# A pad of 128 bytes behind the constants of a two-layer SSD and attention trunk

## The chip, the core and the metric

The kernel runs on one core of one Trainium2 chip. The core has a matrix engine (TensorE, PE in the profile; its weight loads are shown apart as PEld), a vector engine (VectorE, DVE), a scalar engine (ScalarE, ACT), GpSimd (POOL), and a queue processor (SyncE, SP) that here issues nearly all transfers. The transfers are carried by 16 DMA engines from device memory to the on-chip memory of 128 partitions. The metric is the time of one execution on the device in microseconds (us).

## The reference

The model takes `x` (256 tokens by 2048) and a vector `c`, and runs two layers in float32, with one shared key and value projection between them. Cut to what matters:

```python
for layer in range(2):
    shift, scale, gate = split(silu(c) @ ada_w[layer] + ada_b[layer], 3)    # adaLN
    h = x * (1 + scale) + shift
    if layer == 0:   # SSD mixer: 64 heads of 64, 8 groups, state 128
        z, xBC, dt = split(h @ a_in_w)                    # 2048 x 10304
        xs, B, C = split(silu(causal_conv4(xBC)))
        y = ssd_scan(xs * softplus(dt), softplus(dt) * -exp(A_log), B, C) + D * xs
        y = group_rmsnorm(y * silu(z)) * norm_g @ a_out_w  # 4096 x 2048
    else:            # dilated window attention: 3 groups of 8 heads of 128
        q, z = split(h @ b_in_w)                          # 2048 x 4096
        o = merge_by_lse(attention(q_g, k_g, v_g, window_g, dilation_g) for g in 3 groups)
        y = (o * silu(z)) @ b_out_w                       # 1024 x 2048
    x = layer_norm(alpha * x + (1 + gate) * y)
    if layer == 0:
        k, v = split(x @ kv_w)                            # 2048 x 6144, once
```

## The kernel before

Nearly all of the time goes into products of the 256 tokens with float32 weights. Each weight matrix lies in device memory in pieces of 128 partitions by 1024 numbers (4 KB to a partition). A piece is loaded into a tile `raw` (line 89, six buffers), then split into two parts in the matmul format float32r: ACT writes the high part `whi` (line 99) and DVE writes `wlo` = raw - whi (line 101). The activations are split in the same way, and a product is the sum of three matmuls: high by high, high by low, low by high. There are two ways to run it:

- Token-major (`tm_mults`, lines 212 to 214): the activations are the stationary operand and the weights the moving one, 512 columns at a time. The z products of layer 0, `wout`, the v products and `wbout` run so.
- Channel-major: the weights are stationary, and the activations move. In `cm_piece` (lines 150 to 152) 256 columns move in each of the three matmuls. In `cm_wide` (lines 181 and 184) high and low activations lie side by side, so that 512 columns move past the high weights, and then 256 past the low ones. `wxs`, k, q and the gate of layer 1 run so.

The tiles `whi` and `wlo` are 1088 numbers long, and a piece begins at one of two places in them: at number 0 (`LONG`) where it will be the moving operand, or at number 16, 64 bytes further on (`SHORT`), where it will be stationary.

```python
    SHORT, LONG = (16, 16), (0, 0)
    ...
        return [wp.tile([P, 1088], F32R, name=n, bufs=4)[:, o:o + 1024] for n, o in zip(("whi", "wlo"), off)]
    ...
        copied.append(S.activation(hi, raw, AF.Copy))
        ...
            latest.append(V.tensor_tensor(lo, raw, hi.bitcast(F32), op=ALU.subtract))
```

AdaLN is not a matmul. Its weights (96 rows of 1 MB, 8 KB to a partition, tile `araw`, issued at line 287) are multiplied by silu(c), which stands in the constant tile `cb_` on every partition, and summed by one DVE instruction a row (line 294). Layer 0's shift and scale must be known before `h`, so 32 of these rows come first, and the opening of the kernel (to about 160 us) weaves them with the first weight pieces by a list written out by hand. Later rows are worked off in the background between pieces. The order of every engine is the order in which the program issues the work; some instructions are pinned behind others by `tc.issue_after`. All weight and adaLN transfers go through SP's queue, and each waits for its buffer to come free.

The tiles come from pools that lie behind each other in the on-chip memory, each tile at a multiple of 32 bytes. First come the constants (pool `cons`): `cb_` (8192 bytes to a partition), `adab` (384), `prm` (1732), `cc` (1536; identity, triangle, ones), and further on in the code `magic` and the two `mod` tiles of the adaLN results. Behind them lie the weights (`wp`), the activations (`act`), small tiles (`sm`), the slots, and the pools that come and go with the stages. Only the residual `u` (pool `pu`) is laid out from the other end.

```python
    cb_ = cons.tile([P, D], F32, name="cb_")
    ...
    adab_ = cons.tile([P, NB], F32, name="adab")
    prm = cons.tile([P, NPAR - NB], F32, name="prm")
    ...
    cc = cons.tile([P, NCONST], F32, name="cc")
    ...
    ident = cc[:, CI:CI + 128]
    tri = cc[:, CT:CT + 128]
    ones = cc[:, CM:CM + 128]
```

Of the kernel before, what the change touches and what calls it, by code (L numbers as in the profile page):

```python
# [9 lines left out]
F32 = mybir.dt.float32  # L10
# [8 lines left out]
P = 128  # L19
# [30 lines left out]
def trunk(ctx, tc, xT, x, c, par, cst, bias, lnrow, ada, wdt, win, wxs, wout, wk, wv, wbin, wbout, out):  # L50
# [3 lines left out]
    cons = ctx.enter_context(tc.tile_pool(name="cons", bufs=1))  # L54
# [23 lines left out]
    ident = cc[:, CI:CI + 128]  # L78
    tri = cc[:, CT:CT + 128]
    ones = cc[:, CM:CM + 128]  # L80
    SHORT, LONG = (16, 16), (0, 0)

    def rows(t, b):
# [1293 lines left out]
```

## Time and profile before

| | |
|---|---|
| median of 3 runs | 1236.28 us (1235.71 to 1237.11) |
| profiled execution | 1236.29 us, span 1234.5 us |
| granted TensorE clock, mean | 0.999 |
| moved by DMA | 335.92 MB, mean 272 GB/s |
| DMA busy share, main queue | 75.0% of 16 engines |

The span is the time from the first to the last instruction of the profiled execution; 1.8 us of its time lie around it. Busy time of an engine is the time in which at least one of its instructions ran. A row of a group of instructions gives its line, engine, operation, output and inputs, shapes and count, then the busy time and the mean duration of one, then the idle time of the engine just before them. Consecutive matmuls overlap, so the mean duration of one is longer than the distance between two starts. Line numbers are those of the kernel before.

### The profile page before, as it was taken

What the parts mean: (1) busy time and instruction counts of PE and PEld (TensorE: products, weight loads), DVE (VectorE), ACT (ScalarE), POOL (GpSimd) and SP (SyncE); (2) the same over time, 40 slices, a digit from 0 to 9 for tenths busy, and PEclk for the clock granted to TensorE, in tenths of its full rate; (3) what the DMA queues carried; (4) which work ended last, traced back from release to release, by engine and by line L of the source; (5) the groups of instructions that cost most, each with busy time, mean ns of one, the idle gap of its engine ahead of it and who ended that gap; (6) DMA issues with size and microseconds to landing.
All of it is one profiled execution on the core that took longest, in us unless ns stands there. A gap on an engine that the chain in (4) does not pass through costs nothing.

```text
span 1234.5 us, 18854 instructions
## 1 busy us (share of the span) xinstructions
PE 1220.3 (99%) x7132; PEld 1049.4 (85%) x7132; DVE 1028.0 (83%) x1464; ACT 701.6 (57%) x1048; POOL 3.9 (0%) x8
## 2 busy tenths in 40 slices
PE   8999999999999999999999999999999999999998
PEld 7889988898888888888888788888888888888886
DVE  6899996999988989899778678888978876758776
ACT  3554577878597789754335545344445644445551
POOL 0000000000000000000000000000000000000001
PEclk9999999999999999999999999999999999999999
DMA  9999986687666456599998569989998774464673
GB/s 373 414 414 415 413 283 244 216 305 247 222 204 205 171 172 205 203 337 353 365 316 294 195 204 362 356 341 371 378 382 313 224 261 147 122 201 124 207 256 69
DMA packets 81372, 335.92 MB, mean 272 GB/s; under 512 B 9201, under 2 KB 9985, under 8 KB 68481
## 3 DMA queue, kind: packets, MB, share of 16 engines
q1 hardware_dynamic: 80352, 333.33, 75.0%
q0 software_dynamic: 576, 1.05, 0.6%
q8 instruction: 56, 0.92, 0.3%
q10 hardware_dynamic: 352, 0.34, 0.1%
q14 instruction: 36, 0.29, 0.1%
HBM read 331.45 MB, written 3.23 MB: 271 GB/s over the span
## 4 chain that ended last, share of the span: by engine, by line
PE 84%; DMA 6%; DVE 6%; ACT 2%; issue 1%; ACTq 0%; DVEq 0%
PE acc L181 24%; PE acc L184 12%; PE acc L213 12%; PE acc L214 12%; PE acc L212 12%; DMA raw<-in_win 5%; DVE araw L294 3%; DVE wlo L101 2%; PE py L775 1%; PE acc L150 1%; PE acc L152 1%; PE acc L151 1%; DMA araw<-in_ada 1%; ACT whi L99 1%; PE acc L985 1%
## 5 line engine op out<-in xcount | busy, mean ns | idle before, releaser
L99 ACT ACTIVATE whi<-raw 128x1024 fp32r<-128x1024 f32 x389 | 408.9, 1058 | 362.5 <-PE acc L214 130.7
L101 DVE TENSOR_TENSOR wlo<-raw,whi 128x1024 fp32r<-128x1024 f32 x389 | 469.2, 1221 | 146.8 <-ACT whi L99 139.9
L181 PE MATMUL acc<-actT,whi 128*128 128x512 f32 x1280 | 402.8, 394 | 0.0
L184 PEld LDWEIGHTS acc<-actT,wlo 128*128 128x128 f32 x1280 | 239.5, 188 | 53.5 <-DVE wlo L101 0.5
L213 PE MATMUL acc<-wlo,actT 128*128 128x512 f32 x656 | 257.3, 392 | 1.9 <-DVE wlo L101 1.9
L212 PE MATMUL acc<-whi,actT 128*128 128x512 f32 x656 | 254.0, 394 | 0.0
L184 PE MATMUL acc<-actT,wlo 128*128 128x256 f32 x1280 | 253.8, 280 | 0.0
L294 DVE SCALAR_TENSOR_TENSOR araw<-araw,cb__72 128x2048 f32<-128x2048 f32 x95 | 217.0, 2284 | 5.2 <-DMA araw<-in_ada 4.7
L181 PEld LDWEIGHTS acc<-actT,whi 128*128 128x128 f32 x1280 | 193.9, 188 | 0.4
L214 PE MATMUL acc<-whi,actT 128*128 128x512 f32 x432 | 168.8, 391 | 0.0
L213 PEld LDWEIGHTS acc<-wlo,actT 128*128 128x128 f32 x656 | 123.2, 188 | 28.7 <-DVE wlo L101 3.6
L212 PEld LDWEIGHTS acc<-whi,actT 128*128 128x128 f32 x656 | 122.6, 188 | 25.1 <-ACT s L634 0.8
L150 PE MATMUL acc<-actT,whi 128*128 128x256 f32 x372 | 103.7, 283 | 2.9 <-ACT s L634 2.0
L152 PE MATMUL acc<-actT,wlo 128*128 128x256 f32 x372 | 102.4, 283 | 1.7 <-DVE wlo L101 1.6
L151 PE MATMUL acc<-actT,whi 128*128 128x256 f32 x372 | 103.6, 281 | 0.0
L214 PEld LDWEIGHTS acc<-whi,actT 128*128 128x128 f32 x432 | 81.1, 188 | 16.6
L214 PE MATMUL acc<-whi,ylo 128*128 128x512 f32 x224 | 87.6, 391 | 0.0
L150 PEld LDWEIGHTS acc<-actT,whi 128*128 128x128 f32 x372 | 70.3, 190 | 4.2 <-ACT s L634 2.4
L152 PEld LDWEIGHTS acc<-actT,wlo 128*128 128x128 f32 x372 | 69.5, 190 | 2.7 <-DVE wlo L101 2.7
L151 PEld LDWEIGHTS acc<-actT,whi 128*128 128x128 f32 x372 | 71.3, 192 | 0.2
L214 PEld LDWEIGHTS acc<-whi,ylo 128*128 128x128 f32 x224 | 42.1, 188 | 8.7
L733 ACT ACTIVATE seg<-cbc,cumT 128x128 f32<-128x128 f32 x128 | 41.1, 390 | 2.6 <-PE py L775 2.1
(311 smaller groups left out, 1151.1 us busy)
## 6 DMA issues: line engine op xcount, KB each, us to landing
araw<-in_ada SPq DMA_DIRECT2D x96, 1024.0 KB, 7.4
raw<-in_win SPq DMA_DIRECT2D x109, 512.0 KB, 5.7
raw<-in_wout SPq DMA_DIRECT2D x64, 512.0 KB, 5.8
raw<-in_wbin SPq DMA_DIRECT2D x64, 512.0 KB, 4.0
raw<-in_wxs SPq DMA_DIRECT2D x48, 512.0 KB, 4.4
raw<-in_wv SPq DMA_DIRECT2D x48, 512.0 KB, 6.8
raw<-in_wk SPq DMA_DIRECT2D x48, 512.0 KB, 7.2
cbc<-cumd SPq DMA_DIRECT2D x16, 512.0 KB, 4.9
```

What stands on the lines that cost most here:

```text
L99: copied.append(S.activation(hi, raw, AF.Copy))
L101: latest.append(V.tensor_tensor(lo, raw, hi.bitcast(F32), op=ALU.subtract))
L150: T.matmul(o, hi[:, k, c_], ahi[:, kt, :], start=first, stop=False, skip_group_check=True)
L151: T.matmul(o, hi[:, k, c_], alo[:, kt, :], start=False, stop=False, skip_group_check=True)
L152: T.matmul(o, lo[:, k, c_], ahi[:, kt, :], start=False, stop=kt == k1 - 1, skip_group_check=True)
L181: T.matmul(ps[n], hi[:, k, n * P:n * P + P], both(kt), start=kt == 0, stop=False, skip_group_check=True)
L184: T.matmul(ps[n][:, 0, :], lo[:, k, n * P:n * P + P], high(kt), start=False, stop=kt == KT - 1, skip_group_check=True)
L212: T.matmul(o, h_, hi[:, k, :], start=kt == k0, stop=False, skip_group_check=part)
L213: T.matmul(o, h_, lo[:, k, :], start=False, stop=False, skip_group_check=part)
L214: end = T.matmul(o, l_, hi[:, k, :], start=False, stop=kt == k1 - 1, skip_group_check=part)
L294: return V.scalar_tensor_tensor(raw, raw, 1.0, cb_, op0=ALU.mult, op1=ALU.mult, accum_out=mod[layer][:, ct, j:j + 1])
L733: S.activation(seg[:, hh, b, :], cbc[:, hh, b, :], AF.Relu, bias=cumT[:, b, h0 + hh:h0 + hh + 1], scale=-1.0)
```

## The change

One tile of 32 float32 numbers, 128 bytes on each partition, is added to the pool of constants behind `cc`. No instruction writes it or reads it.

```diff
     ident = cc[:, CI:CI + 128]
     tri = cc[:, CT:CT + 128]
     ones = cc[:, CM:CM + 128]
+    cons.tile([P, 32], F32, name="pad")
     SHORT, LONG = (16, 16), (0, 0)
```

Everything that is laid out behind it lies 128 bytes further on. The table gives where tiles begin, as the remainder by 256 bytes:

| tiles | before | after |
|---|---|---|
| `cb_`, `adab`; `prm`; `cc` | 128; 0; 224 | 128; 0; 224 |
| `raw`, `whi` and `wlo` (as tiles), activations `actT`, slots `s0` to `s7` | 128 | 0 |
| stationary weights, at `SHORT` in `whi` and `wlo` | 192 | 64 |
| moving weights, at `LONG` | 128 | 0 |
| `araw`, opening: pool `wp1`; pool `pe` | 128; 192 | 0; 64 |
| `araw`, later | 128 | 0 |
| `xt` and `htmp` of the opening | 192 | 64 |
| `xs`, `cbc`, `seg`, `sz`, `ylo`, `q`, `bs`, `pT`, `sc` | 128 | 0 |
| `u0`, `u1` | 224 | 224 |

The instructions, their order on each engine and queue, their waits and their shapes are the same in both programs; only addresses differ, and each line number behind the pad is larger by one.

## The prediction

> **What bounds the kernel now.** I read the page's first part and the chain first: they say whose time the span is.
>
> ```profile
> span 1234.5 us, 18854 instructions
> PE 1220.3 (99%) x7132; PEld 1049.4 (85%) x7132; DVE 1028.0 (83%) x1464; ACT 701.6 (57%) x1048; POOL 3.9 (0%) x8
> PE 84%; DMA 6%; DVE 6%; ACT 2%; issue 1%; ACTq 0%; DVEq 0%
> ```
>
> TensorE (PE) is busy for 1220.3 of 1234.5 us and makes 84% of the chain; the DMA's 6% and VectorE's (DVE) 6% can only lie where PE is not full. So next come busy times by stretch: the opening in pieces of 20 us, then a stretch of one v product and the wide k products.
>
> ```profile
> 20.00:40.00 20.00, 17.58 (x113) 16.28 (x114) 16.46 (x17) 12.02 (x18) 0.00 (x0) 0.91 1.02 414
> 40.00:60.00 20.00, 19.09 (x135) 17.02 (x135) 18.25 (x21) 9.90 (x14) 0.00 (x0) 1.00 1.02 414
> 60.00:80.00 20.00, 19.21 (x107) 16.36 (x107) 18.88 (x21) 11.65 (x15) 0.00 (x0) 1.00 1.02 413
> 80.00:100.00 20.00, 20.00 (x116) 17.58 (x115) 18.85 (x23) 10.75 (x14) 0.00 (x0) 1.00 1.02 413
> 100.00:120.00 20.00, 20.00 (x127) 18.11 (x126) 18.74 (x20) 10.64 (x15) 0.00 (x0) 1.00 1.02 415
> 120.00:140.00 20.00, 20.00 (x171) 19.85 (x170) 18.72 (x22) 8.49 (x11) 0.00 (x0) 1.00 1.02 414
> 140.00:160.00 20.00, 19.34 (x152) 18.45 (x152) 18.78 (x19) 10.51 (x13) 0.00 (x0) 1.00 1.01 402
> ...
> 740.00:900.00 160.00, 160.00 (x887) 139.03 (x886) 139.14 (x142) 70.70 (x88) 0.00 (x0) 1.00 0.94 361
> ```
>
> The columns are the stretch and its length, then the busy time of PE, weight loads (PEld), DVE, ACT and POOL, the granted clock, the DMA share and GB/s. From 20 to 140 us all sixteen DMA engines are full (share 1.02, 413 to 415 GB/s), yet PE itself is full from 80 to 140. From 740 to 900 PE has no gap at all. So there are two levers only: the pace of a matmul, nearly everywhere, and the transfers, in the opening, by as much as PE lacks there.
>
> A busy PE need not run at one pace, so the third look is at starts in the timeline. The first rows are the wout product (stationary activations, weights as the 512 moving columns), the next the wide k and v product (stationary weights), the last two the first product early and at 59 us.
>
> ```profile
> 600.17 0.39 PE L213 MATMUL acc<-wlo,actT 128*128 128x512 f32 x1
> ...
> 601.08 0.39 PE L214 MATMUL acc<-whi,ylo 128*128 128x512 f32 x1
> ```
>
> ```profile
> 771.37 0.40 PE L184 MATMUL acc<-actT,wlo 128*128 128x256 f32 x2
> ...
> 772.75 0.39 PE L184 MATMUL acc<-actT,wlo 128*128 128x256 f32 x2
> ```
>
> ```profile
> 22.18 0.28 PE L151 MATMUL acc<-actT,whi 128*128 128x256 f32 x1
> ...
> 22.52 0.28 PE L151 MATMUL acc<-actT,whi 128*128 128x256 f32 x1
> ```
>
> ```profile
> 59.34 0.28 PE L150 MATMUL acc<-actT,whi 128*128 128x256 f32 x1
> ...
> 59.81 0.28 PE L151 MATMUL acc<-actT,whi 128*128 128x256 f32 x1
> ```
>
> In wout four matmuls of 512 columns lie between the rows: 0.91 / 4 = 227.5 ns each. At 22 us three of 256 columns take 0.34 us, 113.3 ns each; at 59 us four take 0.47 us, 117.5 ns each. The wide product needs 1.38 / 2 = 690 ns for its set of four (two of 512, two of 256), where the paces above would give 2 x 227.5 + 2 x 113.3 = 681.7. So the same form runs at two paces some 4% apart, without any wait. What chooses between them no row says. That is the unknown of this case.
>
> **The change part by part.** *The pad itself.* Its tile is never written or read: on every engine and queue the same instructions stand in the same order with the same waits. Nothing is added or removed: 0 us, and no cover to lose.
>
> *Addresses of what PE reads.* Weights, activations and the slots move together by 128 bytes. The moving operand starts at 128 over a multiple of 256 now, and at 0 after; stationary weights with the SHORT offset of 64 bytes go from 192 to 64. The distance between the two operands of a matmul stays. The trace has one pair of neighbours: weight loads from 192 (L181, SHORT) and from 128 (L213, stationary activations).
>
> ```profile
> L181 PE MATMUL acc<-actT,whi 128*128 128x512 f32 x1280 | 402.8, 394 | 0.0
> L213 PE MATMUL acc<-wlo,actT 128*128 128x512 f32 x656 | 257.3, 392 | 1.9 <-DVE wlo L101 1.9
> L181 PEld LDWEIGHTS acc<-actT,whi 128*128 128x128 f32 x1280 | 193.9, 188 | 0.4
> L213 PEld LDWEIGHTS acc<-wlo,actT 128*128 128x128 f32 x656 | 123.2, 188 | 28.7 <-DVE wlo L101 3.6
> L151 PE MATMUL acc<-actT,whi 128*128 128x256 f32 x372 | 103.6, 281 | 0.0
> ```
>
> Both loads take 188 ns, and the matmuls around them 394 and 392. No moving operand of these lines starts anywhere but at 128, so the trace can't price the move to 0. The ends are the two paces: every matmul of the slower sort quickened, or every one of the quicker sort slowed. They are worked out as rivals below, about -10.0 and +8.9 us. I take 0, since a shift that both operands share leaves their distance alone and the nearest pair of addresses, 64 bytes apart, shows nothing.
>
> *Addresses of what ACT and DVE read and write.* The split of a weight piece writes wlo at 128 in wout's stretch (LONG) and at 192 in the wide one (SHORT).
>
> ```profile
> L101 DVE TENSOR_TENSOR wlo<-raw,whi x45: 1206/1225/1227, 570.6 to 687.6; 128x1024 fp32r<-128x1024 f32 x45
> ```
>
> ```profile
> L101 DVE TENSOR_TENSOR wlo<-raw,whi x47: 1217/1221/1226, 769.2 to 898.5; 128x1024 fp32r<-128x1024 f32 x47
> ```
>
> ```profile
> L101 DVE TENSOR_TENSOR wlo<-raw,whi 128x1024 fp32r<-128x1024 f32 x389 | 469.2, 1221 | 146.8 <-ACT whi L99 139.9
> ```
>
> The columns of the first two rows are minimum, median and maximum in ns. Medians of 1225 and 1221 ns mean that DVE hardly sees such offsets. If it did, by those 4 ns, 389 splits (the page's row) would be 1.6 us, either way. DVE is busy 83% of the span, so that lies beside matmuls; in the opening, where DVE has less room (16.5 to 18.9 of 20 us), a part of it could show. ACT, busy 57%, has more room than DVE for its half of the split. I put 0 for both.
>
> *Addresses that the transfers write.* Weight pieces (4 KB to a partition) and adaLN rows (8 KB) land at 128, the adaLN rows in the second pool of the opening at 192; after, at 0 and 64. Two short stretches hold almost nothing on the main queue but 8 KB rows, first into the pool at 128, then into that at 192.
>
> ```profile
> DMA packets 196, 0.83 MB, mean 415 GB/s; under 512 B 99, under 2 KB 99, under 8 KB 99
> q1 hardware_dynamic: 106, 0.79, 93.9%
> ```
>
> ```profile
> DMA packets 86, 0.64 MB, mean 426 GB/s; under 512 B 8, under 2 KB 8, under 8 KB 8
> q1 hardware_dynamic: 86, 0.64, 101.3%
> ```
>
> The first is 5.2 to 7.2 us: 196 - 99 = 97 rows of 8 KB in 0.939 x 16 x 2.0 = 30.0 us of engine time, 310 ns each. The second is 12.8 to 14.3 us: 86 - 8 = 78 rows in 1.013 x 16 x 1.5 = 24.3 us, 312 ns each. Moving the landing place by 64 bytes changes 0.6% at most. A landing at 0 is in neither. The ends: no gain, or all that PE lacks from 20 to 160 us, 140 - 135.22 (the sum of the seven rows) = 4.8 us and 9% of the clock for 20 us, 1.8 us, together -6.6 us. I take 0, by the pair of rows, which is nearest. Behind 160 us PE lacks little or other engines make the gap, and a quicker transfer is hidden by PE.
>
> The Trainium skill speaks for a gain here, in "DMA: Bandwidth & Descriptors", section "How a descriptor splits into AXI transactions": a descriptor that does not begin at a multiple of 256 bytes has its first transaction begin at the boundary below, and bytes that are fetched unused still cost beats. By its count a 4 KB row at 128 takes 132 beats where an aligned one takes 128, 3.0%, and an 8 KB row 260 for 256, 1.5%; at the opening's mixture some 2% of 140 us, an estimate of 3 us. By the rows the sum has 0 there. By the same count the row at 192 would be 0.8% dearer than that at 128, and 312 against 310 ns neither shows nor excludes that.
>
> The sum is 0. The profiled execution took 1236.29 us, its span 1234.5 and 1.8 around it; the median of the runs is 1236.28. I predict 1236.3 us.
>
> **The rivals.** *Quicker transfers (faster).* If landing at 0 makes rows 2% quicker, between the 0.6% of the pair and the 4.7% (6.6 of 140 us) behind which nothing is left to win, the full queue from 20 to 160 us delivers the last piece 2.8 us sooner, and PE's gaps can take it in: 1233.5 us. Over 0.2% it is worth from 1.8% on. Against it: half of the stretch has PE full already. This is the rule of the Trainium skill above.
>
> *PE at its quicker pace everywhere (faster).* The wide product would gain 690 - 681.7 = 8.3 ns for 1280 / 2 = 640 sets, 5.3 us; the first product at most 4.2 ns for 3 x 372 matmuls, 4.7 us. Together 10.0 us: 1226.3 us. For it: both paces exist without waits. Against it: the distance of the operands stays.
>
> *PE loses its quick pace (slower).* In wout's beginning the product of L212 to L214 runs slower without a wait:
>
> ```profile
> 545.43 0.40 PE L212 MATMUL acc<-whi,actT 128*128 128x512 f32 x1
> ...
> 546.59 0.39 PE L214 MATMUL acc<-whi,ylo 128*128 128x512 f32 x1
> ```
>
> Five take 1.16 us, 232 ns each and not 227.5. If reading moving rows from 0, or LDWEIGHTS from 0 and 64, brings this pace to all of them, 3 x 656 matmuls of actT alone pay 4.5 ns each: 8.9 us, 1245.2 us. It decides from 1.3 ns a matmul on (2.5 us over 1968). PE is full there, so nothing hides it. For it: these lines run at the quicker pace nearly everywhere, so a disturbance has more to take than to give. Against it: as before, the shared shift.
>
> **How the numbers follow.** 0.2% (2.5 us) is about what a measurement of this kernel can tell from no change. No effect has 0.38; quicker transfers 0.20, of which 0.13 beyond 0.2%; the quick pace 0.10; the lost pace 0.32, as its place is the largest and fully exposed. So faster 0.13 + 0.10 = 0.23, slower 0.32, the same 0.38 + 0.07 = 0.45. The range runs from 1228 us, below the whole transfer case and with the milder half of the quick pace, to 1248 us, above the lost pace with a little for the first product; some 0.15 is left out. The likeliest case alone has 1234 to 1238.5.
>
> **What would show it.** No effect: starts 227 to 228 ns apart in wout and 690 ns a set in the wide product, the opening's stretches at 413 to 415 GB/s and PE at 135 of 140 us from 20 to 160. Quicker transfers: more GB/s there at the same share, and PE gaps at 20 to 80 us shorter. The pace: other distances between starts in stretches where PE has no gap. I would be wrong if matmul starts move while operations of ACT and DVE keep their durations, or if the opening's transfers carry over 422 GB/s (2% more).

## The result, and the profile after

| | before | after |
|---|---|---|
| median of 22 runs each | 1236.30 us (1235.56 to 1237.94) | 1234.41 us (1233.01 to 1235.55) |
| ratio | 1 | 0.9984, 95% interval 0.9978 to 0.999 |
| profiled execution | 1236.29 us, span 1234.5 | 1235.14 us, span 1233.4 |

The pad makes the kernel 0.16% quicker, 1.9 us: small, but outside what the runs leave uncertain. The profiled execution of after is one of its slower ones, so its rows show 1.1 us of gain and not 1.9.

The stretches of the opening, in the columns of the prediction:

```profile
20.00:40.00 20.00, 19.00 (x135) 17.59 (x136) 17.68 (x20) 12.40 (x19) 0.00 (x0) 1.00 1.02 422
40.00:60.00 20.00, 17.78 (x121) 15.60 (x120) 19.01 (x22) 10.71 (x17) 0.00 (x0) 1.00 1.02 420
60.00:80.00 20.00, 19.95 (x111) 17.36 (x112) 18.51 (x20) 12.42 (x16) 0.00 (x0) 1.00 1.02 421
80.00:100.00 20.00, 20.00 (x113) 17.50 (x112) 18.73 (x20) 10.36 (x14) 0.00 (x0) 1.00 1.02 422
100.00:120.00 20.00, 20.00 (x134) 18.38 (x133) 18.89 (x21) 10.22 (x13) 0.00 (x0) 1.00 1.02 424
120.00:140.00 20.00, 19.93 (x170) 19.73 (x169) 18.88 (x21) 9.42 (x12) 0.00 (x0) 1.00 1.02 422
140.00:160.00 20.00, 19.34 (x152) 18.45 (x151) 18.74 (x22) 10.81 (x14) 0.00 (x0) 1.00 0.95 377
```

At the same share (1.02) the queue carries 420 to 424 GB/s where it carried 413 to 415, and from 140 us on the share falls to 0.95, since the backlog is worked off sooner. So the transfers are 2% quicker. The main queue from 60 to 140 us, first before, then after, says the same in engine time:

```profile
q1 hardware_dynamic: 7218, 33.01, 101.7%
```

```profile
q1 hardware_dynamic: 7346, 33.68, 101.7%
```

1.017 x 16 x 80 = 1302 us of engine time carry 33.01 MB before, 39.4 us per MB, and 33.68 MB after, 38.7.

Where the time goes is seen best by the same six matmuls in both programs: the first behind the wait at 30 us, one 4 us later, the first of the z product at 47 us, one at 140 us, the first of the SSD stage's transposes, and one in wout. Before:

```profile
32.25 0.38 PE L150 MATMUL acc<-actT,whi 128*128 128x256 f32 x1 [1.95 <-ACT s L634]
...
35.97 0.37 PE L150 MATMUL acc<-actT,whi 128*128 128x256 f32 x1
...
47.63 0.63 PE L212 MATMUL acc<-whi,actT 128*128 128x512 f32 x2
...
140.98 0.38 PE L152 MATMUL acc<-actT,wlo 128*128 128x256 f32 x1 [0.54 <-DVE wlo L101]
...
224.38 0.63 PE L744 MATMUL aux<-cc,xs 128*128 128x128 f32 x4 [0.67 <-DVE cb L723]
...
580.45 0.39 PE L213 MATMUL acc<-wlo,actT 128*128 128x512 f32 x1
```

After (line numbers larger by one):

```profile
30.98 0.38 PE L151 MATMUL acc<-actT,whi 128*128 128x256 f32 x1 [0.56 <-ACT s L635]
...
33.25 0.28 PE L151 MATMUL acc<-actT,whi 128*128 128x256 f32 x1
...
46.19 0.63 PE L213 MATMUL acc<-whi,actT 128*128 128x512 f32 x2
...
138.21 0.38 PE L153 MATMUL acc<-actT,wlo 128*128 128x256 f32 x1
...
222.91 0.63 PE L745 MATMUL aux<-cc,xs 128*128 128x128 f32 x4 [1.57 <-DVE cb L724]
...
579.40 0.50 PE L214 MATMUL acc<-wlo,actT 128*128 128x512 f32 x1 [0.38 <-DVE wlo L102]
```

The lead is 1.27, then 2.72, 1.44, 2.77, 1.47 and 1.05 us. The first 1.3 us are the shorter wait (0.56 for 1.95 us). The next 1.4 are the clock: 0.91 from 20 to 40 us before, 1.00 after; matmuls of 256 columns took 0.2 us each there, and 0.12 now. By 47 us this much is lost again. The lead grows back at later waits for pieces, to 2.2 us from 60 to 120 us and to 2.77 at 141, where PE waits 0.54 us for `wlo` before and shows no such wait after. Behind the opening PE gives 1.7 us of it back, most of that in longer waits for DVE (`cb` in the SSD stage, a `wlo` in wout).

The pace of the matmuls, the other lever, has not moved. First wout, then the wide k product, both after:

```profile
600.39 0.39 PE L213 MATMUL acc<-whi,actT 128*128 128x512 f32 x1
...
601.30 0.39 PE L214 MATMUL acc<-wlo,actT 128*128 128x512 f32 x1
```

```profile
771.19 0.62 PE L182 MATMUL acc<-actT,whi 128*128 128x512 f32 x2
...
772.58 0.62 PE L182 MATMUL acc<-actT,whi 128*128 128x512 f32 x2
```

0.91 / 4 = 227.5 ns and 1.39 / 2 = 695 ns a set, at the view's rounding the 227.5 and 690 of before. Over all starts of the two traces that no pause follows, the means agree to 0.1 ns (token-major products 227.6 and 227.5; wide 230.9 and 230.9 for 512 columns, 116.0 and 116.0 for 256).

### The profile page after: what moved, and what is told of

Its sections match the earlier page's. It is cut to its first block, busy times and chain, and to the rows that moved or that the text cites. A ratio compares the mean times of both kernels' runs of the same rounds, so it can differ in the third digit from the quotient of the medians.

```text
span 1233.4 us, 18854 instructions
## 1 busy us (share of the span) xinstructions
PE 1219.2 (99%) x7132; PEld 1048.7 (85%) x7132; DVE 1027.8 (83%) x1464; ACT 701.2 (57%) x1048; POOL 3.9 (0%) x8
## 3 DMA queue, kind: packets, MB, share of 16 engines
q0 software_dynamic: 576, 1.05, 0.6%
## 4 chain that ended last, share of the span: by engine, by line
PE 81%; DMA 10%; DVE 6%; ACT 2%; issue 1%; DVEq 0%; ACTq 0%; SPq 0%
PE acc L182 24%; PE acc L185 12%; PE acc L214 11%; PE acc L215 11%; PE acc L213 11%; DMA raw<-in_win 5%; DMA araw<-in_ada 3%; DVE wlo L102 2%; DVE araw L295 2%; PE py L776 1%; ACT whi L100 1%; PE acc L151 1%; PE acc L153 1%; PE acc L152 1%; PE acc L986 1%
## 5 line engine op out<-in xcount | busy, mean ns | idle before, releaser
L100 ACT ACTIVATE whi<-raw 128x1024 fp32r<-128x1024 f32 x389 | 408.5, 1058 | 358.7 <-PE acc L215 128.9
L102 DVE TENSOR_TENSOR wlo<-raw,whi 128x1024 fp32r<-128x1024 f32 x389 | 469.2, 1220 | 147.8 <-ACT whi L100 139.1
```

## The experiments

**Which move does it?** The theory after the result: the transfers of the opening are quicker because what they write begins at 0 by 256 (A), by the weight pieces (A1) or by the adaLN rows (A2). The rival: any move of the tiles does it (C).

A pad of twice the size moves everything and keeps every remainder:

```diff
+    cons.tile([P, 64], F32, name="pad")
```

> The pad is 256 bytes and not 128, so every tile behind the constants moves, but its remainder by 256 stays what it was before (weights, activations and slots at 128, adaLN rows of the opening at 128 and 192). Theory A, the remainder by 256 of what the transfers write decides: as before, 1236.3 us, and 413 to 415 GB/s from 20 to 140 us. Theory C, any move of the tiles does it, since other places in the memory collide: as the changed kernel, 1234.4 us and 420 to 424 GB/s.

Measured: 1236.24 us, ratio to before 0.9997 (0.9988 to 1.0006). C falls.

Weight pieces alone:

```diff
+    cons.tile([P, 32], F32, name="pad")
...
+        if not back:
+            back.append(wp.tile([P, 32], F32, name="back", bufs=1))
         return [wp.tile([P, 1088], F32R, name=n, bufs=4)[:, o:o + 1024] for n, o in zip(("whi", "wlo"), off)]
```

> The pad stays, and a second one of 128 bytes stands in the weight pool behind the six buffers of raw pieces, so that raw alone begins at multiples of 256; whi, wlo, activations, slots and adaLN rows keep the remainders of before (128, and 192 for the adaLN rows of the second pool). If the weight pieces make the gain (theory A1): 1234.4 us and 420 GB/s or more in the opening. If the adaLN rows make it (theory A2): 1236.3 us and 414 GB/s. If both share it by their transactions, 17 for 16 in a 4 KB row and 33 for 32 in an 8 KB one: about 418 GB/s and 1235.2 us.

Measured: 1234.33 us, 0.9983 (0.9974 to 0.9992), the whole gain. Since here whi, wlo, activations and slots have the remainders of before, the gain owes nothing to what PE reads. ACT and DVE do read `raw`, but a split is no quicker for it (DVE 1225 ns on the mean for 1221 before, ACT 1059 for 1058).

The adaLN rows without the weight pieces, at 0 in the first pool and 64 in the second (the pools behind them move too):

```diff
             wp1 = cS.enter_context(tc.tile_pool(name="wp1", bufs=2))
+            wp1.tile([P, 32], F32, name="pad", bufs=1)
```

> No pad behind the constants; one of 128 bytes at the head of the first pool of adaLN rows instead, so that the adaLN rows of the opening (and the pools behind them) go from 128 and 192 to 0 and 64, while weights, activations and slots stay at 128. Theory A1 (weight pieces): 1236.3 us and 414 GB/s from 20 to 140 us. Theory A2 (adaLN rows): 1234.4 us and 420 GB/s or more. Both by halves: about 418 GB/s and 1235.2 us.

Measured: 1236.29 us, 0.9999 (0.9989 to 1.0008). The stretch from 20 to 140 us of before, after, double pad, weight pieces alone and adaLN rows alone, one row each:

```profile
20.00:140.00 120.00, 115.88 (x758) 105.19 (x759) 109.91 (x118) 63.45 (x85) 0.00 (x0) 0.99 1.02 414
```

```profile
20.00:140.00 120.00, 116.67 (x775) 106.16 (x776) 111.70 (x120) 65.54 (x88) 0.00 (x0) 1.00 1.02 422
```

```profile
20.00:140.00 120.00, 115.20 (x760) 104.79 (x760) 110.27 (x118) 63.93 (x86) 0.00 (x0) 0.99 1.02 414
```

```profile
20.00:140.00 120.00, 116.15 (x773) 105.44 (x774) 111.89 (x121) 66.14 (x89) 0.00 (x0) 1.00 1.02 422
```

```profile
20.00:140.00 120.00, 115.64 (x766) 104.66 (x767) 110.83 (x119) 65.20 (x87) 0.00 (x0) 1.00 1.02 417
```

GB/s stand last: 414, 422, 414, 422, 417. So weight pieces make the gain (A1), but the adaLN rows, half of them at 0, made 3 of the 8 GB/s too, and in time nothing that can be told.

**What of other remainders?** Three more pads:

```diff
+    cons.tile([P, 16], F32, name="pad")
```

> The pad is 64 bytes: weight pieces land at 192 and not 128, the adaLN rows of the opening at 192 and 0 and not 128 and 192; nothing of 4 KB is aligned to 256. If only a remainder of 0 gives the quicker transfers and the weight pieces carry it: 414 GB/s and 1236.3 us. If 128 is the one bad remainder (a row split into halves of a transaction at both ends): 420 GB/s or more and 1234.4 us. If the aligned adaLN rows of the second pool alone help: 415 to 418 GB/s, 1235.5 us.

Measured: 1235.65 us, 0.9989 (0.998 to 0.9999), 418 GB/s from 20 to 140 us.

```diff
+    cons.tile([P, 8], F32, name="pad")
```

> The pad is 32 bytes: weight pieces land at 160, adaLN rows of the opening at 160 and 224. If each transfer of a piece that begins inside a 256-byte block just has one block more, any remainder but 0 is alike: 414 GB/s from 20 to 140 us and 1236.3 us. If the remainder counts by how much of the first block is left over (64 bytes at 192 gave 418 GB/s, 128 bytes at 128 gave 414), 96 bytes at 160 lie between: 415 to 417 GB/s and 1236 us.

Measured: 1236.13 us, 1.0 (0.9991 to 1.0009), 414 GB/s.

```diff
+    cons.tile([P, 48], F32, name="pad")
```

> The pad is 192 bytes: weight pieces land at 64, adaLN rows of the opening at 64 and 128. The mirror of the 64-byte pad (192 bytes of the first block are used, 64 of the last). If the unevenness of the two end blocks decides: as with the 64-byte pad, 417 to 419 GB/s and 1235.6 us. If only 0 is quick and all else equal: 414 GB/s, 1236.3 us.

Measured: 1236.31 us, 0.9998 (0.9989 to 1.0007), 414 GB/s. With the weight pieces at 160, 128 or 64 the queue is alike. The 64-byte pad stands out, and it is the only one of the three that puts adaLN rows at 0 (the second pool's, as the adaLN run did with the first pool's, for 417 GB/s). That fits a gain which takes rows at 0, while the distance from 0 of the others does not count; weight pieces at 192 without aligned adaLN rows were not tried.

The 32-byte pad shows something else. Its opening, from 20 to 80 us:

```profile
20.00:40.00 20.00, 18.14 (x129) 16.73 (x130) 17.05 (x17) 12.04 (x18) 0.00 (x0) 1.00 1.02 415
40.00:60.00 20.00, 18.46 (x128) 16.31 (x126) 18.59 (x24) 9.90 (x15) 0.00 (x0) 1.00 1.02 413
60.00:80.00 20.00, 19.14 (x107) 16.44 (x106) 18.88 (x20) 12.39 (x17) 0.00 (x0) 1.00 1.02 414
```

In this execution the wait at 30 us happened to be 1.4 us, the clock stayed at 1.00, and at 36 us it led the one of before by 2.0 us, as after did by 2.7. At 107 us the lead was 0.3, at 580 us 0.1. PE lost it in waits for `wlo`, whose pieces come through a queue still at 414 GB/s. The 192-byte pad has the better clock too, behind a wait even longer than that of before, and no gain:

```profile
32.80 0.39 PE L151 MATMUL acc<-actT,whi 128*128 128x256 f32 x1 [2.38 <-ACT s L635]
```

```profile
20.00:40.00 20.00, 17.34 (x121) 15.44 (x121) 16.04 (x18) 11.61 (x19) 0.00 (x0) 1.00 1.02 414
```

So the better clock at 30 us is not what holds the gain; the queue's rate is.

**Does alignment of all rows add anything?** The changed kernel with one tile widened, so that the second pool's adaLN rows go from 64 to 0:

```diff
-                crow2 = pe.tile([48, P + KT], F32R, name="crow", bufs=1)
+                crow2 = pe.tile([48, 192], F32R, name="crow", bufs=1)[:, :P + KT]
```

> The pad stays, and one small tile of the second adaLN pool is widened from 576 to 768 bytes, so that its adaLN rows and the x rows of the opening begin at 0 too, where the changed kernel has them at 64. Weight pieces carry the gain, so nothing more is left to win if they do it alone: 1234.4 us and 422 GB/s. If the adaLN rows still add their part: 425 GB/s and 1233.7 us.

Measured: 1235.0 us, 0.9988 (0.9979 to 0.9997), 422 GB/s. Nothing more. And the other way round, all adaLN rows (and the x rows of the opening) at 0 and weight pieces left at 128:

```diff
+            wp1.tile([P, 32], F32, name="pad", bufs=1)
...
+                crow2 = pe.tile([48, 192], F32R, name="crow", bufs=1)[:, :P + KT]
```

> The kernel before with pads in the two pools of adaLN rows alone, so that all adaLN rows and the x rows of the opening land at 0 (0 and 64 in the earlier run with 417 GB/s), weights and activations at 128 as before. If adaLN rows do their share by how many of them are aligned: 420 GB/s and 1235.2 us. If rows that begin in the middle of a block slow the whole queue as long as any of them is left: 417 GB/s as in that run, 1236.3 us.

Measured: 1235.4 us, 0.9991 (0.9982 to 1.0), and the queue in full:

```profile
20.00:140.00 120.00, 116.60 (x776) 105.96 (x777) 111.71 (x120) 65.36 (x88) 0.00 (x0) 1.00 1.02 421
```

I had not expected that: for the queue it does not matter which of the two kinds is at 0, one is enough for 421 or 422 GB/s, half of one gives 417 or 418, none 414. In time this run gains only 0.9 us, and its interval reaches no change: in the profiled execution PE led by 2.9 us at the matmul of 141 us, as after by 2.8, and gave 1.4 of it back by 224 us and more behind.

The queue's slower rate in the opening belongs to two kinds of rows in flight together, neither at a multiple of 256. That alone does not make it. From 740 to 900 us both kinds are in flight too, at 128 before and at 0 after; the main queue there, before and after:

```profile
q1 hardware_dynamic: 11778, 57.59, 93.6%
```

```profile
q1 hardware_dynamic: 11844, 58.01, 94.5%
```

0.936 x 16 x 160 / 57.59 = 41.6 us of engine time per MB before, and 41.7 after: no gain where the queue is not quite full. What makes the opening differ, and why a place at 0 helps there, is open.

**Is the opening's length the transfers'?** The changed kernel with 1 MB more to carry there:

```diff
+                spare_row = pe.tile([P, 1024], F32, name="spare", bufs=1)
...
                     fetch_piece()
+                    if i in (1, 5):
+                        nc.sync.dma_start(spare_row, wout[0][i])
```

> The changed kernel with two more transfers of 512 KB in the opening (a tile that nobody reads; one early, at the second piece of the list, one at the sixth). At 422 GB/s they take 1.05 MB / 422 = 2.5 us of the full queue, about what the alignment saves over the opening. If the opening's length is the transfers' (theory A): the gain is gone, 1236 to 1237 us, PE's busy time from 20 to 160 us back to that of before. If the gain was not in the queue but in the shorter wait at 30 us and the clock kept there: 1234.4 us as long as the clock stays at 1.00.

Measured: 1236.97 us, 1.0001 (0.9992 to 1.001): the gain is gone, with the clock at 1.00 from 20 to 40 us and the queue at 422 GB/s.

```profile
20.00:160.00 140.00, 133.47 (x900) 120.89 (x901) 128.16 (x137) 74.11 (x98) 0.00 (x0) 1.00 1.01 419
```

PE is busy for 133.5 us of that stretch, 135.2 before. 2.5 us of transfers cost 2.1 us by the ratios (1.0001 for 0.9984) and 2.6 by the medians. Each ratio is uncertain by about 1 us; within that, a microsecond of the queue in the opening is one of the kernel.

**Larger blocks, and a surprise.** Weight pieces at multiples of 4096 bytes:

```diff
+    cons.tile([P, 72], F32, name="pad")
...
-    magic = cons.tile([P, 2], I32, name="magic")
+    magic = sm.tile([P, 2], I32, name="magic", bufs=1)
...
-    mod = [cons.tile([P, KT, 3], F32, name=f"mod{i}") for i in range(2)]
+    mod = [sm.tile([P, KT, 3], F32, name=f"mod{i}", bufs=1) for i in range(2)]
```

> The two small tiles of the adaLN results and one constant move from the pool of constants to that of small tiles, and a pad of 288 bytes stands in their place: the weight pieces begin at multiples of 4096 bytes (before 128, in the changed kernel 256 over a multiple of 512), whi, wlo and activations at 0 by 256, slots and later pools at 160, adaLN rows of the opening at 160 and 224. If 256 bytes is the whole grain: as the changed kernel, 421 to 422 GB/s and 1234.4 us. If larger blocks count too: 425 GB/s or more and 1233.5 us. If pools at 160 cost ACT, DVE or PE anything, it is slower than 1235 us with the transfers as quick.

Measured: 1239.93 us, 1.0026 (1.0016 to 1.0036), slower, with 421 GB/s in the opening. A larger block adds nothing to the transfers. Most of the loss lies in wout: from its first matmul with `ylo` to its last it takes 178.2 us here and 174.4 after, 3.8 of the 4.7 us between the two spans; where the rest arises is not shown.

```profile
599.88 0.40 PE L215 MATMUL acc<-whi,ylo 128*128 128x512 f32 x1
...
601.28 0.40 PE L215 MATMUL acc<-whi,ylo 128*128 128x512 f32 x1
```

Six matmuls in 1.40 us are 233 ns each, where before and after have 227.5. In this kernel the weights that move are at 0 and `ylo`, stationary in every third matmul, at 160. So PE can lose its pace without a wait, as the prediction's slower rival has it, here by a move that the operands do not share. To test it, the changed kernel with `ylo` alone moved (and what lies behind it in its pool):

```diff
         pn = cA.enter_context(tc.tile_pool(name="pn", bufs=1, reuse_waits="tile"))
+        pn.tile([P, 40], F32, name="pad")
```

> The changed kernel with a pad of 160 bytes at the head of the pool that holds ylo, the low half of y, stationary in every third matmul of wout: it begins at 160 by 256, while whi, wlo and the other activations stay at 0. In the run with raw at multiples of 4096 ylo lay at 160 too, and wout's matmuls came 233 ns apart and not 227. If the distance between stationary and moving operand sets the pace: 233 ns again, 4 to 5 us over 660 matmuls, 1239 us. If the slots at 160 made it there: 227 ns and 1234.4 us.

Measured: 1238.15 us, 1.001 (1.0001 to 1.002).

```profile
659.92 0.39 PE L213 MATMUL acc<-whi,actT 128*128 128x512 f32 x1
...
663.42 0.39 PE L213 MATMUL acc<-whi,actT 128*128 128x512 f32 x1
```

Fifteen in 3.50 us, 233 ns again, and 3.7 us more than after by the medians. All three matmuls of a set are slower, not only the one with `ylo`. That it is the place 160 by itself is excluded by the 32-byte pad, where `ylo` and the moving weights both begin at 160:

```profile
599.98 0.39 PE L213 MATMUL acc<-whi,actT 128*128 128x512 f32 x1
...
603.38 0.39 PE L213 MATMUL acc<-whi,actT 128*128 128x512 f32 x1
```

Fifteen in 3.40 us, 227 ns. And the stationary weights without their 64 bytes:

```diff
-    SHORT, LONG = (16, 16), (0, 0)
+    SHORT, LONG = (0, 0), (0, 0)
```

> The changed kernel with SHORT set to (0, 0), so that stationary weights begin at 0 by 256 and not at 64, at the same remainder as the activations that move past them. If the distance of the operands sets the pace, the wide products and the first product slow down, by 5 to 10 ns a matmul of 256 columns: 640 sets of four at 710 ns and not 690 are 13 us, 1247 us. If only the place of each operand by itself counts, nothing says that 0 is worse than 64: 1234 us.

Measured: 1238.42 us, 1.0014 (1.0005 to 1.0023). The wide product here:

```profile
770.63 0.63 PE L182 MATMUL acc<-actT,whi 128*128 128x512 f32 x2
...
772.73 0.63 PE L182 MATMUL acc<-actT,whi 128*128 128x512 f32 x2
```

Three sets in 2.10 us are 700 ns each, 695 after. The direction was right, the size a third: over all starts that no pause follows, the first product's matmuls come 119.8 ns apart (116.7 after), the wide product's 233.1 (230.9) for 512 columns and 115.4 (116.0) for 256. By 3 x 372, 1280 and 1280 matmuls that is 3.5 + 2.8 - 0.8 = 5.5 us, and 4.0 were measured. Stationary weights at 0 are not slow by themselves: with the 64-byte pad they begin at 0 too, the moving ones at 192, and the paces are 115.7, 230.9 and 116.0 ns. So the place of an operand against the other counts, by up to 3% of a matmul, and once in the other direction (116.0 to 115.4).

## Why the prediction was wrong

The forecast was no change; the kernel is 1.9 us quicker. The measured time lies in the range, and the rival of quicker transfers is what happened.

- *The step that failed* is "Addresses that the transfers write", the 0 "by the pair of rows, which is nearest". Its bound was good (0 to -6.6 us), its choice was not. The two stretches compare rows at 128 with rows at 192, both off the grain, and each was almost alone in its queue. The same stretches after the change, where the rows land at 0 and 64:

```profile
DMA packets 198, 0.84 MB, mean 420 GB/s; under 512 B 100, under 2 KB 100, under 8 KB 100
q1 hardware_dynamic: 103, 0.80, 94.9%
```

```profile
DMA packets 85, 0.63 MB, mean 421 GB/s; under 512 B 8, under 2 KB 8, under 8 KB 8
q1 hardware_dynamic: 85, 0.63, 99.6%
```

  98 rows in 0.949 x 16 x 2.0 us and 77 in 0.996 x 16 x 1.5 us are 310 ns each, as before at 128. A lone row is no quicker at 0, so the pair could not have shown the effect: what the runs show is a gain where weight pieces and adaLN rows mix in a full queue, as in the stretches of 414 GB/s. The term measured 2% of the queue's time there, and 1.9 us of the kernel's.

- *The price of the quicker transfers* was 2.8 us for 2%, the share of the queue that was also measured (422 for 414). The lead at 141 us was 2.77 us; that it is so near is partly chance, for at the same matmul the runs with weight pieces alone, all rows and adaLN rows at 0 led by 2.6, 3.2 and 2.9. Unseen by the price was that PE gives part of it back behind the opening: in the profiled execution 1.3 us by 223 us (0.9 of it in a wait for DVE of 1.57 us for 0.67) and 0.4 by 580 us. How much differs between executions: that of the run with weight pieces alone still led by 2.95 us at 221 us. Of 2.8 us, 1.9 arrive by the medians.

- *The objection to that rival*, that PE is full in half of the stretch, was weak: the lead is kept through the full stretch (2.1 us at 80 us, 2.2 at 120), and what the queue does there decides the wait of the next gap. The run with more bytes shows that the opening's transfers count.

- *The rule of the Trainium skill* ("DMA: Bandwidth & Descriptors", "How a descriptor splits into AXI transactions") pointed the right way, and its 2% for the mixture is what came. It speaks of bytes that are fetched, and the prediction carries it over to the place of landing. As a count of beats it does not fit the runs: by it 4 KB rows at 128 would cost 3% whatever lies beside them, but with the adaLN rows at 0 they run at 421 GB/s, and a lone 8 KB row takes 310 ns at 128 and at 0.

- *PE's pace*: 0 was right, and so was the reason, that operands which move together keep their distance. The three runs that changed the distance show that PE can lose its pace by it: with `ylo` moved, 6 ns a matmul, where 4.5 were priced, over one product and 3.7 us, where three times as many matmuls were priced at 8.9. For this change the rival's 0.32 was too much, since the distance stays. The row that it was priced from is something else: the same five matmuls are slow after the change too (543.89 to 545.04 us, 230 ns each), and a few later the pace is 227 in both. Nor does the distance explain the first product's two paces: at 22 us it has 113 ns before and 117 after (21.85 to 23.02 us, ten starts), with the distance unchanged. What chooses there stays open. Two readings were coarse: the wide set's 690 ns is 693.6 on the mean of the trace, so the quicker rival's 8.3 ns a set should have been 12, and the slower rival's 1968 matmuls take in 224 with `ylo`.

- *ACT and DVE*: 0 was right (a split takes DVE 1221 ns before and 1220 after, ACT 1058 and 1058). *The pad itself*: 0 was right (the 256-byte pad gives 0.9997).

- Of what would show it: the opening's 420 to 424 GB/s are the sign that was named for the quicker transfers, and PE's gaps from 20 to 80 us are shorter (3.3 for 4.1 us). The limit, over 422 GB/s, was set so that only one of the six stretches passes it.

## What to carry to other kernels

Where a stage is bound by transfers of more than one kind at once and the queue is full, place what they write at multiples of 256 bytes, by a dead tile if need be; where they are hidden it was worth nothing here (the lead is 0.9 us at 700 us and 1.1 at 1200). A shared shift of all tiles left the matmuls as they were in each of five pads, but a pad in front of one operand only can cost more than the transfers gain (3.7 us against 1.9 here), so check the remainders of both operands of each product after any change of the layout. A price for an operation alone need not hold for the same operation in a crowd, as the lone rows at 310 ns show: take it from the stage that is to be changed.

## What was not expected of the hardware

- A transfer's landing place counted only in company and in a full queue: from 20 to 140 us 414 GB/s with weight pieces and adaLN rows both off multiples of 256 bytes, 421 or 422 with either kind on them, 417 or 418 with half of one kind; but 310 ns for a lone 8 KB row at 128 and at 0, and 41.6 and 41.7 us of engine time per MB for the mixture at a share of 94%.
- Alignment to 4096 bytes gives no more than 256 (421 GB/s from 20 to 140 us).
- The place of the stationary operand against the moving one bears on a matmul's pace: 512 columns come every 227 ns with both at 0 or both at 160, and every 233 ns when `ylo`, in one of three, is at 160 and the weights at 0; its two neighbours are slowed with it. That 256 bytes is the period is not shown.
- A wait of 1.95 us at 30 us was followed by a granted clock of 0.91 in its 20 us, waits of 0.56, 1.4 and 2.38 us at that place by one of 1.00: the length of the wait alone does not decide it.
